# A gated short-convolution layer on one core: half of the weight remainders of the two-tile stage made by an adding DMA

## The chip, the core and the metric

The kernel runs on one core of a Trainium2 chip. The metric is the device time in microseconds of one execution. Engines are named as in the profile: PE multiplies matrices, PEld is its weight load, DVE, ACT and POOL are the vector, scalar and general engines, and SP issues most of the DMAs. "L314" is line 314 of the kernel before.

## The reference

With 256 tokens, a width of 2048 and a branch width of 4096, the reference does one layer: a normalisation with a modulation taken from a conditioning vector, a wide projection into four parts, a causal convolution of width three, two gates, a projection back, a gated residual and a second normalisation. Cut to what matters:

```python
h = rmsnorm(x, norm_g)
h, gate = adaln(h, c, ada_w, ada_b)              # h * (1 + scale) + shift
proj = einsum('bsd,de->bse', h, w_in)            # 2048 -> 4 * 4096
b_gate, c_gate, v, g = split(proj, 4)
u = causal_depthwise_conv(c_gate * v, conv_w)    # width 3
y = b_gate * u * silu(g)
x = x + gate * einsum('bse,ed->bsd', y, w_out)   # 4096 -> 2048
return rmsnorm(x, final_g)
```

All data is fp32. The kernel multiplies in the rounded type fp32r and keeps the accuracy by splitting each operand into a high part (the rounded value) and a low part (what the rounding left): a product is hi·hi + hi·lo + lo·hi.

## The kernel before, in words

The projection `w_in` is worked off in two stages, and the output projection is a third.

- The first stage (`mm_s` in the profile) takes the first 16 of the 32 column tiles of each quarter of `w_in`, four tiles at a time, in an order that a small planner writes out beforehand (`plan()`), together with the sums for the modulation. It ends at about 380 us of the span.
- The two-tile stage (`mm_b`), which the change touches, takes the other 16 column tiles of each quarter two at a time: `for ct in range(NS, NCT, 2)` makes 8 rounds, and in each the four quarters follow one another (`for q in QUARTERS`). One quarter of one round needs a slab of 2048 x 256 numbers of `w_in`, and it comes as two pieces of 1 MB (`for kp in range(0, KT, KP)` with `KP = 8`): the first piece has the upper 1024 rows (`kp == 0`), the second the lower 1024. So there are 64 pieces, 32 of them second ones.
- The output projection (`mm_o`) follows from about 730 us on.

A piece passes through four places in the two-tile stage. SP loads it into a tile `raw`. ACT rounds it to `hi` (`split_hi`, L314), DVE subtracts to get `lo = raw - hi` (`split_lo`, L319), and PE does 48 products of 128x128 weights and 256 tokens with it, two column tiles by 8 row blocks by 3 products, in the order hi, hi, lo for each block (`product`, L444). Then the quarter's PSUM bank is taken up by ACT or DVE (L595 to L606).

Each of the three kinds of tile has three buffers that turn round (`raw_tile`, `hi_tile`, `lo_tile`, each with `bufs=3`). So `hi` and `lo` of a piece can be written only when PE has ended the piece three back, and a `raw` load can start only when its old content has been read by both ACT and DVE. Inside this stage the order of the instructions on each engine is made by the framework's scheduler, by priorities and by its own idea of when things are ready; PE, ACT, DVE, POOL and SP each run their own list strictly in order and wait for semaphores.

Of the kernel before, what the change touches and what calls it, by code (L numbers as in the profile page):

```python
# [10 lines left out]
AF = mybir.ActivationFunctionType  # L11
ALU = mybir.AluOpType

P = 128
# [16 lines left out]
SLOT = 2048  # L31
# [86 lines left out]
def short_conv_layer(ctx: ExitStack, tc: tile.TileContext, x, c, norm_g, ada_w, ada_b, w_in, conv_w, w_out, final_g, out):  # L118
    nc = tc.nc
# [19 lines left out]
    def raw_tile(name):  # L139
        return wpool.tile([P, SLOT], F32, tag="raw", name=name, bufs=3)  # L140
# [165 lines left out]
    def hi_tile():  # L306
        return wpool.tile([P, SLOT], F32R, tag="hi", name="hi", bufs=3)

    def lo_tile(lo_tag="lo"):
        return wpool.tile([P, SLOT], F32R, tag=lo_tag, name="lo", bufs=3)  # L310

    def split_hi(raw, n, hi=None):
        hi = hi_tile() if hi is None else hi
        nc.scalar.copy(hi[:, :n], raw[:, :n])  # L314
        return hi

    def split_lo(raw, n, hi, lo_tag="lo", lo=None):
        lo = lo_tile(lo_tag) if lo is None else lo
        nc.vector.tensor_tensor(out=lo[:, :n], in0=raw[:, :n], in1=hi[:, :n].bitcast(F32), op=ALU.subtract)  # L319
        return hi, lo  # L320
# [13 lines left out]
    def split(raw, n, lo_tag="lo"):  # L334

        return split_lo(raw, n, split_hi(raw, n), lo_tag)
# [48 lines left out]
    def conv(ct, u, cv):  # L385

        nc.scalar.activation(u, cv, AF.Copy, scale=cw[:, 64 + ct : 65 + ct])
        nc.vector.scalar_tensor_tensor(
            out=u[:, 1:T], in0=cv[:, 0 : T - 1], scalar=cw[:, 32 + ct : 33 + ct], in1=u[:, 1:T], op0=ALU.mult, op1=ALU.add
        )  # L390
        nc.vector.scalar_tensor_tensor(
            out=u[:, 2:T], in0=cv[:, 0 : T - 2], scalar=cw[:, ct : ct + 1], in1=u[:, 2:T], op0=ALU.mult, op1=ALU.add
        )

    def split_y(dst, y):
        nc.scalar.copy(dst[:, :, 0, :], y)
        nc.vector.tensor_tensor(out=dst[:, :, 1, :], in0=y, in1=dst[:, :, 0, :].bitcast(F32), op=ALU.subtract)
# [42 lines left out]
    def product(dst, hi, lo, k, i, begins, left, ends):  # L440

        w, h = ((hi, hh_), (hi, hl_), (lo, hh_))[i]

        mm = last_mm[0] = nc.tensor.matmul(dst, w, h[:, k], start=begins and left, stop=ends, skip_group_check=True)  # L444
        if begins and left:
            opener[0] = mm
        elif begins:
            tc.add_manual_dep(mm.ins, opener[0].ins.name, after, reason="the bank's flags are cleared first")
# [97 lines left out]
    def gate_piece():  # L546
        if not gate_todo:
            return
        dc, j = gate_todo.pop(0)
        at = adap.tile([P, ASLOT], F32, tag="at", name="at_g", bufs=4)  # L550
        at3 = at.rearrange("p (k f) -> p k f", k=2)
        with later(GIVE):
            gate_sums(dc, j, at3)
# [17 lines left out]
    KP = 8  # L571
    n_piece = 0
    for ct in range(NS, NCT, 2):
        for q in QUARTERS:
            bank = psum.tile([P, CT, T], F32, tag="mm", name="mm_b")[:, 0:2]
            col = q * E + ct * P
            for kp in range(0, KT, KP):
                raw = raw_tile("raw")
                nc.sync.dma_start(
                    raw.rearrange("p (k f) -> p k f", k=KP),  # L580
                    w_in[0, kp * P : (kp + KP) * P, col : col + 2 * P].rearrange("(k p) f -> p k f", p=P),
                )
                hi, lo = split(raw, SLOT)
                for m in range(2):
                    for i in range(KP):
                        k = kp + i
                        o = slice((i * 2 + m) * P, (i * 2 + m + 1) * P)
                        for j in range(3):
                            product(bank[:, m, :], hi[:, o], lo[:, o], k, j, k == 0 and j == 0, m == 0, k == KT - 1 and j == 2)
                n_piece += 1  # L590
                if n_piece % 2 == 0:
                    gate_piece()
            z = zs[q // 2][:, q % 2]
            if q == 1:
                nc.scalar.copy(z, bank)  # L595
                zc = z
            elif q == 2:
                nc.vector.tensor_tensor(out=zc, in0=bank, in1=zc, op=ALU.mult)
                for j in range(2):
                    conv(ct + j, z[:, j, :], zc[:, j, :])  # L600
                u = z
            elif q == 3:
                nc.scalar.activation(z, bank, AF.Silu)
                nc.vector.tensor_tensor(out=u, in0=u, in1=z, op=ALU.mult)
            else:
                nc.vector.tensor_tensor(out=u, in0=bank, in1=u, op=ALU.mult)  # L606
                split_y(ys[ct // 2], u)
# [43 lines left out]
    for dc in range(4):  # L651
# [10 lines left out]
        for ep in range(n_ep):  # L662

            first = dc == 0 and ep == 0
            raw = wpool.tile([P, SLOT], F32, tag="raw" if first else "lo", name="raw_o", bufs=3)
# [10 lines left out]
            hi, lo = split(raw, SLOT, "raw")  # L676
# [55 lines left out]
```

## Time and profile before

| | before |
|---|---|
| time of the two runs | 913.66 us and 913.24 us (median 913.45 us) |
| the profiled execution's span, first to last instruction | 911.9 us |
| PE busy, instructions | 895.7 us (98%), 7047 |
| DVE busy, instructions | 616.2 us (68%), 593 |
| ACT busy, instructions | 464.6 us (51%), 413 |
| POOL busy, instructions | 0.7 us, 6 |
| HBM read | 224.49 MB |

The profile is of one execution; of that execution itself it gives the span, and the median of the two timed runs is 1.55 us above it. Busy time is summed per engine over the whole span. A PE that is busy all the time does not say that it is at its peak, but an engine that is never idle in a stage is one that no other engine has made wait there. In the views a row "A <- B" under waits means that A stood idle until B was done.

### The profile page before, as it was taken

Reading aid. Unit: us, or ns where it says so; the run is one execution under the profiler, and the core shown is the slowest. Engines: PE = TensorE matmul, PEld = TensorE weight load, DVE = VectorE, ACT = ScalarE, POOL = GpSimd, SP = SyncE. Lnnn points to the kernel's source line nnn. Section 1 sums busy time; section 2 is a strip of 40 time slices with the busy share of each in tenths; the row PEclk is TensorE's granted clock in tenths of the full one; section 3 lists DMA queues with packets and bytes.
Section 4 is the critical chain, followed back from the end, with each engine's and each line's share of the span. In section 5 each row is a group of like instructions: output and inputs, shape, how many; then the busy total and the mean of one; then the engine's idle time right before and its main releaser. Section 6 shows DMA issues by size and latency. Waiting matters only on the chain.

```text
span 911.9 us, 16239 instructions
## 1 busy us (share of the span) xinstructions
PE 895.7 (98%) x7047; PEld 858.5 (94%) x7047; DVE 616.2 (68%) x593; ACT 464.6 (51%) x413; POOL 0.7 (0%) x6
## 2 busy tenths in 40 slices
PE   6999999999999999999999999999999999999996
PEld 4999999999999999999999999999999988888885
DVE  4889999989888899765545555545554544555882
ACT  6768856665558756743334433444333333443333
POOL 0000000000000000000000000000000000000000
PEclk9999999999999999999999999999999999999998
DMA  9999999999998698676656665566656486655542
GB/s 309 367 371 353 365 325 351 356 369 352 338 328 275 197 359 301 201 246 197 186 188 197 200 201 186 187 195 200 200 188 188 140 331 231 203 201 186 185 139 92
DMA packets 163752, 227.65 MB, mean 250 GB/s; under 512 B 5680, under 2 KB 104160, under 8 KB 163296
## 3 DMA queue, kind: packets, MB, share of 16 engines
q1 hardware_dynamic: 163552, 226.56, 74.8%
q8 instruction: 55, 0.90, 0.4%
q14 instruction: 17, 0.14, 0.0%
q10 hardware_dynamic: 128, 0.04, 0.0%
HBM read 224.49 MB, written 2.10 MB: 248 GB/s over the span
## 4 chain that ended last, share of the span: by engine, by line
PE 94%; DMA 3%; ACT 1%; SPq 1%; DVE 0%; issue 0%; ACTq 0%
PE mm_b L444 38%; PE mm_s L444 36%; PE mm_o L631 6%; PE mm_o L629 6%; PE mm_o L630 6%; DMA raw_s<-in_sc_w_in_dram 2%; DMA at<-in_ada_w_dram 1%; SPq L210 1%; DMA x<-in_x_dram 1%; ACT hi L314 0%; PE ps_gate L568 0%; PE tp_g L434 0%; ACT acc L465 0%; DVE lo L319 0%; ACT hT L300 0%; SPq L413 0%
## 5 line engine op out<-in xcount | busy, mean ns | idle before, releaser
L444 PE MATMUL mm_s<-hT,hi 128*128 128x256 f32 x2048 | 350.5, 277 | 0.2
L444 PE MATMUL mm_b<-hT,hi 128*128 128x256 f32 x2048 | 348.8, 276 | 0.0
L444 PEld LDWEIGHTS mm_s<-hT,hi 128*128 128x128 f32 x2048 | 308.7, 188 | 1.1 <-ACT hT L300 0.4
L444 PEld LDWEIGHTS mm_b<-hT,hi 128*128 128x128 f32 x2048 | 308.7, 188 | 0.2 <-issue 0.2
L444 PE MATMUL mm_b<-hT,lo 128*128 128x256 f32 x1024 | 282.6, 276 | 0.0
L444 PE MATMUL mm_s<-hT,lo 128*128 128x256 f32 x1024 | 282.2, 277 | 0.2 <-DVE lo L319 0.2
L319 DVE TENSOR_TENSOR lo<-raw,hi 128x2048 fp32r<-128x2048 f32 (+1 forms) x66 | 148.0, 2244 | 136.8 <-ACT hi L314 136.8
L314 ACT CAST hi<-raw 128x2048 fp32r<-128x2048 f32 (+1 forms) x66 | 123.7, 1874 | 200.2 <-PE mm_b L444 156.1
L444 PEld LDWEIGHTS mm_b<-hT,lo 128*128 128x128 f32 x1024 | 192.2, 188 | 0.2 <-issue 0.2
L444 PEld LDWEIGHTS mm_s<-hT,lo 128*128 128x128 f32 x1024 | 191.7, 188 | 0.7 <-DVE lo L319 0.6
L319 DVE TENSOR_TENSOR lo<-raw_s,hi 128x2048 fp32r<-128x2048 f32 (+1 forms) x80 | 147.6, 1850 | 25.6 <-ACT hi L314 24.6
L314 ACT CAST hi<-raw_s 128x2048 fp32r<-128x2048 f32 (+1 forms) x80 | 124.2, 1559 | 72.0 <-PE mm_s L444 59.2
L319 DVE TENSOR_TENSOR lo<-raw_o,hi 128x2048 fp32r<-128x2048 f32 x32 | 73.3, 2292 | 66.3 <-ACT hi L314 66.1
L314 ACT CAST hi<-raw_o 128x2048 fp32r<-128x2048 f32 x32 | 61.0, 1907 | 107.2 <-PE mm_o L631 83.7
L630 PE MATMUL mm_o<-lo,y 128*128 128x512 f32 x256 | 99.7, 391 | 0.0
L629 PE MATMUL mm_o<-hi,y 128*128 128x512 f32 x256 | 99.3, 389 | 0.0
L631 PE MATMUL mm_o<-hi,y 128*128 128x512 f32 x256 | 99.3, 389 | 0.0
L427 DVE SCALAR_TENSOR_TENSOR gv<-at,silu_c,gv 128x512 f32<-128x512 f32 x105 | 78.6, 749 | 2.2 <-DMA at<-in_ada_w_dram 0.3
L465 ACT COPY acc<-mm_s 128x1024 f32<-128x1024 f32 x54 | 54.5, 1012 | 35.9 <-PE mm_s L444 35.9
L630 PEld LDWEIGHTS mm_o<-lo,y 128*128 128x128 f32 x256 | 48.1, 188 | 10.2 <-issue 0.2
L631 PEld LDWEIGHTS mm_o<-hi,y 128*128 128x128 f32 x256 | 48.0, 188 | 10.2 <-issue 0.2
L629 PEld LDWEIGHTS mm_o<-hi,y 128*128 128x128 f32 x256 | 48.1, 188 | 9.9
(89 smaller groups left out, 349.6 us busy)
## 6 DMA issues: line engine op xcount, KB each, us to landing
raw<-in_sc_w_in_dram SPq DMA_DIRECT2D x64, 1024.0 KB, 5.7
raw_s<-in_sc_w_in_dram SPq DMA_DIRECT2D x47, 1024.0 KB, 7.9
raw_o<-in_sc_w_out_dram SPq DMA_DIRECT2D x32, 1024.0 KB, 5.1
at<-in_ada_w_dram SPq DMA_DIRECT2D x114, 256.0 KB, 8.0
raw_s<-in_sc_w_in_dram SPq DMA_DIRECT2D x33, 512.0 KB, 7.1
at_g<-in_ada_w_dram SPq DMA_DIRECT2D x32, 512.0 KB, 7.8
at<-in_ada_w_dram SPq DMA_DIRECT2D x6, 512.0 KB, 9.6
x<-in_x_dram SPq DMA_DIRECT2D x4, 512.0 KB, 6.4
```

The source lines that it names most:

```text
L210: nc.sync.dma_start(at[:, :, s, :], adas[:, j : j + kk, s, 0 : NK0 * P])
L314: nc.scalar.copy(hi[:, :n], raw[:, :n])
L319: nc.vector.tensor_tensor(out=lo[:, :n], in0=raw[:, :n], in1=hi[:, :n].bitcast(F32), op=ALU.subtract)
L427: nc.vector.scalar_tensor_tensor(out=gv, in0=at4[:, i], scalar=c_k, in1=gv, op0=ALU.mult, op1=ALU.add)
L444: mm = last_mm[0] = nc.tensor.matmul(dst, w, h[:, k], start=begins and left, stop=ends, skip_group_check=True)
L465: nc.scalar.copy(acc[ch, q], bank)
L629: nc.tensor.matmul(po, yh, hi[:, o], start=opens, stop=False, skip_group_check=True)
L630: nc.tensor.matmul(po, yh, lo[:, o], start=False, stop=False, skip_group_check=True)
L631: nc.tensor.matmul(po, yl, hi[:, o], start=False, stop=ct == NCT - 1, skip_group_check=True)
```

## The change

In the two-tile stage the first piece of each quarter is handled as before. For the second piece (`kp` = 8) ACT writes `hi` as before, and then a second ACT instruction writes the rounded value once more, with the sign turned, into `lo`. A DMA that POOL issues then reads the same 1 MB of `w_in` from HBM a second time and adds it to what stands in `lo`, so that `lo` = -hi + raw. DVE's subtraction for these 32 pieces is gone. `lo` of a second piece is now written by ACT and then by the DMA, and PE's products with it wait for the DMA. Tiles, buffer counts and the loads by SP are as before.

```diff
                 raw = raw_tile("raw")
-                nc.sync.dma_start(
-                    raw.rearrange("p (k f) -> p k f", k=KP),
-                    w_in[0, kp * P : (kp + KP) * P, col : col + 2 * P].rearrange("(k p) f -> p k f", p=P),
-                )
-                hi, lo = split(raw, SLOT)
+                w_piece = w_in[0, kp * P : (kp + KP) * P, col : col + 2 * P].rearrange("(k p) f -> p k f", p=P)
+                nc.sync.dma_start(raw.rearrange("p (k f) -> p k f", k=KP), w_piece)
+                if kp == 0:
+                    hi, lo = split(raw, SLOT)
+                else:
+                    hi, lo = split_hi(raw, SLOT), lo_tile()
+                    nc.scalar.activation(lo, raw, AF.Copy, scale=-1.0)
+                    nc.gpsimd.dma_start(lo.rearrange("p (k f) -> p k f", k=KP), w_piece, accum_op=ALU.add)
```

## The prediction

> **What bounds the kernel now.** I read the page first, for the whole span: which engine is busy, and the chain of work that ended last.
>
> ```profile
> span 911.9 us, 16239 instructions
> PE 895.7 (98%) x7047; PEld 858.5 (94%) x7047; DVE 616.2 (68%) x593; ACT 464.6 (51%) x413; POOL 0.7 (0%) x6
> ...
> PE 94%; DMA 3%; ACT 1%; SPq 1%; DVE 0%; issue 0%; ACTq 0%
> ```
>
> The chain lies on PE for 94% of the span and on DVE for none, although DVE is busy for 68% of it. The change is confined to the two-tile stage, so I then asked for busy times by windows: first the stage, and below it a stretch early in the kernel, where the DMA engines are fullest. The columns are the window, its length, the busy time of PE, PEld, DVE, ACT and POOL with counts, the granted clock, the DMA share and GB/s.
>
> ```profile
> 380.00:729.00 349.00, 349.00 (x3076) 348.52 (x3076) 185.15 (x138) 142.21 (x106) 0.00 (x0) 1.00 0.61 194
> 20.00:60.00 40.00, 39.62 (x343) 38.88 (x342) 34.69 (x44) 30.66 (x39) 0.00 (x0) 1.00 1.07 368
> ```
>
> PE is busy in all 349.0 us of the stage, its weight load in 348.5, at the full clock. One product takes 349 / 3076 = 113.5 ns, and a piece of 48 products 5.45 us. DVE has 164 us of idle time in the stage and ACT 207. So nothing that is taken off DVE there can shorten the stage by more than half a microsecond; the question is whether the new way of making `lo` keeps up.
>
> How much room it has is read from the waits in this window and from ACT's timeline.
>
> ```profile
> ACT hi L314 <- PE mm_b L444: 162.6, 49, 4.4
> DVE lo L319 <- ACT hi L314: 138.7, 62, 3.1
> ...
> 478.32 1.91 ACT L314 CAST hi<-raw 128x2048 fp32r<-128x2048 f32 x1 [3.53 <-PE mm_b L444]
> 480.14 0.57 ACT L595 COPY z<-mm_b 128x512 f32<-128x512 f32 x1
> 483.72 1.91 ACT L314 CAST hi<-raw 128x2048 fp32r<-128x2048 f32 x1 [3.00 <-PE mm_b L444]
> 489.16 1.91 ACT L314 CAST hi<-raw 128x2048 fp32r<-128x2048 f32 x1 [3.53 <-PE mm_b L444]
> ```
>
> ACT's rounding waits for PE, not for the load: a `hi` buffer comes free when PE ends the piece three back, every 5.4 us (478.32, 483.72, 489.16), and the raw data is there. From that moment to PE's own use two whole pieces pass. Before, 1.91 us of ACT and 2.29 us of DVE had to fit into them, which leaves more than half of the room unused.
>
> **The change part by part.** What is removed and what ACT is given:
>
> ```profile
> L319 DVE TENSOR_TENSOR lo<-raw,hi 128x2048 fp32r<-128x2048 f32 x62 | 142.1, 2292 | 133.1 <-ACT hi L314 133.1
> L314 ACT CAST hi<-raw 128x2048 fp32r<-128x2048 f32 x62 | 118.6, 1913 | 197.3 <-PE mm_b L444 156.1 <-issue 40.7 <-PE mm_s L444 0.5
> ```
>
> DVE loses 32 subtractions of 2.29 us, 73 us; its stage sum falls from 185 to 112 us and the time gains nothing, because PE covers all of it. ACT gains 32 negated copies. Their shape and source are those of the rounding, so I take its 1.91 us: 61 us more, 142 to 203 of 349 us. That is hidden as a sum, but each copy stands ahead of the adding DMA and counts in its latency. Behind it in ACT's list stands the next piece's `hi`, which must wait for PE a piece longer anyway. The raw buffer is released by the copy instead of DVE's subtraction, 1.9 instead of 2.3 us after `hi`, so SP's loads start no later.
>
> The order of the changed program, which can be read without running it, moves PE's work as well. From about the tenth quarter on it repeats over two quarters: the first piece of quarter A (48 products), two `hi` products of A's second piece, 37 products of B's first piece, the other 46 of A's second piece, the last 11 of B's first, and the 48 of B's second. The earlier quarters interleave in a similar way. So A's second piece gets a late start, and B's second piece none.
>
> Now the room for each adding DMA, counted in PE's products. B's second piece takes the buffers of A's first piece, free after product 48, and its first `lo` product is number 146 (144 before it, two with `hi`): 98 products, 11.1 us. A's second piece takes the buffers of the previous B's first piece, free after product 144, and its `lo` is due at 192 + 87 = 279: 135 products, 15.3 us. ACT's `hi` (1.82 us from its start to the next instruction's in the timeline above) and the negated copy (1.91 us) come off both. What is left for POOL's wake-up, its issuing, the transfer and the semaphore is 7.4 us in the tight case and 11.6 us in the loose one. Call this latency L.
>
> If L is over 7.4 us, PE waits L - 7.4 us at B's second piece, once in two quarters, 16 times in 32 quarters. Every product behind it waits too, the next first piece with all its data ready among them, since PE's list is in order. That wait lengthens the loose room by as much, so the loose case never waits. The cost is 16 x (L - 7.4) us.
>
> L itself has no row, since no DMA in this trace adds and none comes from POOL. The nearest rows are SP's loads of the very same pieces, and the DMA queue in this window:
>
> ```profile
> L579 SPq DMA_DIRECT2D raw<-in_sc_w_in_dram x64: 367/368/379, 357.4 to 701.1; - x64
> ...
> DMA to landing us min/median/max: 5.3/5.7/9.7
> ...
> DMA packets 64300, 67.54 MB, mean 194 GB/s; under 512 B 1040, under 2 KB 62480, under 8 KB 64272
> ## 3 DMA queue, kind: packets, MB, share of 16 engines
> q1 hardware_dynamic: 64272, 67.11, 60.8%
> ```
>
> From below, the adding transfer cannot land sooner than a plain load of the same bytes in the same queues, 5.3 us: it would then be hidden and cost 0, and no gain lies below that since PE has no idle time to give. From above, take the slowest plain load, 9.7 us, twice, because the add needs the old `lo` from SBUF beside the new bytes from HBM: 19.4 us, or 16 x 12.0 = 192 us. Between them I take two median loads, 2 x 5.7 = 11.4 us: two reads for one write, and a queue that is shared with SP's loads. That gives 16 x (11.4 - 7.4) = 64 us.
>
> The Trainium skill's page "Collectives: The Full Stack", section "Why ReduceScatter is half of AllGather", says that an add in a DMA engine costs two read descriptors for each chunk and so half the rate, which is the doubling that I chose; no run here shows it yet. Its page "DMA: Bandwidth & Descriptors", section "Anatomy of one DMA — SWDGE (gpsimd) path", fits a POOL-issued DMA as 2.0 us plus its bytes at 436 GB/s: as an estimate 4.4 us for a plain megabyte and 6.8 us with the bytes counted twice, which would be hidden. The trace is against the fit's premise of free engines: its plain loads take 5.7 us with the engines 61% busy.
>
> The DMA engines set a second limit. The queue row gives 349 x 16 x 0.608 / 64272 = 52.8 ns for one packet of about 1 KB. The 32 adding DMAs bring 32 x 1024 = 32768 more of these. At one price each they need 108 us beside the 212 us of now, 320 of 349 us, and fit. At two they need 216 us, together 428 us: 79 us too many. With the full engines' price (368 GB/s in the early window, 16 engines, 44.5 ns) the same two come to 179 + 182 = 361 us, 12 us too many. These 12 and 79 us lie on both sides of the 64 us from the latency. They are another view of the same waits, so I do not add them.
>
> Issuing on POOL costs no one else anything, since POOL has no other work in the stage (0.00 us in the window). SP's list of loads keeps its order there.
>
> The sum is made against the profiled span: 911.9 + 64 = 976 us, and with the 1.55 us by which the median of the runs is above that span, **978 us**.
>
> **The rivals.**
>
> *Hidden.* The add's second read overlaps with the first, or the transfer's share of the engines is better than I think, and L stays under 7.4 us at both places. For it: a plain load lands in 5.3 to 5.7 us, and the DMA engines are idle for 39% of the stage. Against it: only 1.7 us would be left for the second read and for POOL's part. PE stays full and the time is 913 to 915 us; up to L = 8.5 us it would still be within 2%.
>
> *POOL is slow at issuing the rows.* Each of these DMAs has 1024 rows of 1 KB, and POOL has to issue them, which it does nowhere in this trace. Only one general instruction of POOL is there to price it:
>
> ```profile
> masks.py:199 POOL TENSOR_SCALAR_AFFINE_SELECT ident<-ident 128x128 f32<-128x128 f32 x1 | 0.3, 294 | 0.1
> ```
>
> That is 2.3 ns for an element; with 1024 rows and three records for each (two reads, a write) it makes 7.1 us. L would be 18.5 us, the cost 16 x 11.1 = 178 us and the time 1091 us. For it: nothing in the chain hides it. Against it: SP's issue of the same rows takes 0.37 us, and POOL may run ahead of the transfer.
>
> *The clock falls in the new waits.* After the last product, at about 904.4 us, the granted clock is
>
> ```profile
> 905.00:912.00 7.00, 0.00 (x0) 0.00 (x0) 1.31 (x3) 1.83 (x5) 0.00 (x0) 0.60 0.60 213
> ...
> 0.00:5.00 5.00, 0.26 (x1) 0.18 (x1) 0.17 (x2) 2.01 (x3) 0.70 (x6) 1.00 0.58 184
> ```
>
> If it falls to half, a mean of 0.60 means that it fell 2 us after PE stopped. Sixteen waits of 4 us could each be followed by some 2 us at half speed, losing 1 us each: 978 + 16 = 994 us. Against it: in the first 5 us of the kernel, the second row, PE is idle for 4.7 us and the clock stands at 1.00. The Trainium skill's page "TensorE: Matmul & The Clock Gate", section "Part 1: The HAM clock gate", says that an idle window of about 3.4 us halves the clock until another such window has been busy; that would be 1.7 us lost for each wait, as an estimate 27 us, and the end of this trace agrees that it falls.
>
> *Faster.* A shorter chain by way of DVE's relief would need a wait of PE on DVE in this stage, and PE has none; I give it the smallest chance.
>
> **How the numbers follow.** Waits of about 4 us at every second quarter, 978 us (own range 940 to 1030): 0.51. Hidden: 0.20. POOL slow or the add much dearer, around 1091 us: 0.18. The same as the forecast, with a falling clock, around 994 us: 0.10. Faster: 0.01. For eight times in ten I leave out half of the hidden case at the lower end and half of the slow case at the upper end: 918 to 1110 us. About 2% either way, 18 us, is what a measurement of this kernel can tell from no change. Within it lies the hidden case, 0.20; slower is the sum of the three others, 0.79; faster by more than that is 0.01.
>
> **What would show it right or wrong.** In the profile after, the waits should name PE on the DMA into `lo` about 16 times in the two-tile stage, for some 4 us each and 64 us together, and none of PE on DVE. The issue list should show 32 DMAs of 1 MB from POOL with a median of about 11 us to landing; 7 us or less is the hidden case, and 18 or more the slow one. ACT should show 32 negated copies of 1.9 us, and DVE's subtractions of `raw` should be 32 fewer. POOL's rows show whether its issuing takes tenths of a microsecond or several. The windows should keep the clock at 1.00, and the DMA share of the stage should rise to 0.9 or more. I am wrong about the mechanism if PE waits at every second piece instead of every other one, or if the waits fall on SP's `raw` loads.

## The result, and the profile after

The changed kernel takes 1026.42 us (two runs, 1026.39 and 1026.45) against 913.45 us: a ratio of 1.123, 95% interval 1.121 to 1.125. It is slower by 113 us; the forecast was slower by 64. The head of its page:

```profile
span 1024.7 us, 16353 instructions
PE 934.4 (91%) x7047; PEld 893.5 (87%) x7047; DVE 543.3 (53%) x561; ACT 520.9 (51%) x445; POOL 50.5 (5%) x38
...
PEclk9999999999999998898999898989999989999999
```

The last line needs care. It is the granted clock of PE in 40 slices of the span, and before the change it was

```profile
PEclk9999999999999999999999999999999999999998
```

After, the two-tile stage is a mixture of 9 and 8. PE makes the same 7047 products and is busy 38.7 us longer (934.4 - 895.7). The span grew by 112.8 us; the other 74 must be idle time of PE. The groups and the waits say where:

```profile
L444 PE MATMUL mm_b<-hT,lo 128*128 128x256 f32 x1024 | 297.7, 293 | 74.8 <-DMA lo<-in_sc_w_in_dram 65.5
...
PE mm_b L444 <- DMA lo<-in_sc_w_in_dram: 65.5, 14, 5.4
PE mm_b L444 <- ACT lo L585: 9.3, 2, 4.7
```

Ahead of `lo` products PE is idle for 74.8 us in 14 + 2 = 16 waits, none on DVE. The two that are put down to ACT's copy are of the same size and place; the DMA is what follows that copy. So 74.8 + 38.7 = 113.5 us accounts, within a microsecond, for the 112.8 us of the span. One of the waits, in the timelines of ACT, POOL and PE (start, duration, engine; the bracket is the idle time before):

```profile
580.07 1.91 ACT L585 ACTIVATE lo<-raw 128x2048 fp32r<-128x2048 f32 x1
...
582.34 1.55 POOL L586 DMA_DIRECT2D lo<-in_sc_w_in_dram  x1 [15.95 <-ACT lo L585]
...
588.94 0.28 PE L444 MATMUL mm_b<-hT,lo 128*128 128x256 f32 x1
589.05 0.39 PE L444 MATMUL mm_b<-hT,hi 128*128 128x256 f32 x2
594.05 0.40 PE L444 MATMUL mm_b<-hT,lo 128*128 128x256 f32 x1 [4.61 <-DMA lo<-in_sc_w_in_dram]
594.25 0.63 PE L444 MATMUL mm_b<-hT,hi 128*128 128x256 f32 x2
```

The copy ends at 581.98, and PE starts at 594.05: L is 12.1 us where 11.4 was taken, and 12.1 - 7.4 = 4.7 us fits the wait of 4.61. Behind it a product takes 0.40 us in the records where one ahead of it takes 0.28. By windows of 3.4 us across the wait before this one, and behind this one (us, PE, PEld, DVE, ACT, POOL, granted clock, DMA share, GB/s):

```profile
560.20:563.60 3.40, 0.00 (x0) 0.00 (x0) 2.89 (x2) 3.40 (x4) 0.00 (x0) 0.99 1.14 180
563.60:567.00 3.40, 2.16 (x10) 2.19 (x11) 0.00 (x0) 0.88 (x1) 1.55 (x1) 0.50 0.90 262
567.00:570.40 3.40, 3.40 (x18) 3.40 (x18) 0.00 (x0) 0.00 (x0) 0.00 (x0) 0.51 0.96 285
570.40:573.80 3.40, 3.40 (x32) 3.40 (x32) 0.00 (x0) 0.94 (x1) 0.00 (x0) 1.00 1.17 220
...
577.20:580.60 3.40, 3.40 (x33) 3.40 (x32) 0.00 (x0) 2.34 (x2) 0.00 (x0) 1.00 0.69 183
...
594.20:597.60 3.40, 3.40 (x17) 3.40 (x18) 0.00 (x0) 0.00 (x0) 1.57 (x1) 0.50 0.95 293
597.60:601.00 3.40, 3.40 (x32) 3.40 (x31) 0.00 (x0) 0.00 (x0) 0.00 (x0) 0.99 0.98 264
```

PE stands still for 4.7 us, then does 18 products in 3.4 us where 32 is usual, and the clock is back at 1.00 after 570. Behind the first wait two windows have half clock, behind the second one. Over the stage, 8 of the 16 waits have two such windows behind them and 8 have one, by the trace's clock records. The DMA share is 1.14 in the wait, but 1.17 again at 570.4 with PE busy, and 0.69 at 577.2. A share above 1 says that the recorded times of packets overlap, so it does not say by itself that nothing more would fit. The whole stage, its DMA queues, and the landing of the loads after:

```profile
380.00:848.30 468.30, 393.51 (x3105) 388.47 (x3104) 117.83 (x110) 200.03 (x142) 49.83 (x32) 0.91 0.95 218
...
q1 hardware_dynamic: 64800, 68.16, 49.1%
q0 software_dynamic: 33280, 33.56, 45.4%
...
raw<-in_sc_w_in_dram SPq DMA_DIRECT2D x60, 1024.0 KB, 6.6
lo<-in_sc_w_in_dram POOLq DMA_DIRECT2D x32, 1024.0 KB, 13.2
...
L586 POOL DMA_DIRECT2D lo<-in_sc_w_in_dram x32 | 49.8, 1557 | 775.0 <-ACT lo L585 775.0
```

The stage lasts 468 us instead of 349, and its DMA share rose from 0.61 to 0.95. Over 468 us on 16 engines, one packet of the adding queue (q0) takes 468 x 16 x 0.454 / 33280 = 102 ns, and one of SP's queue 56.7 ns (52.8 before): an adding packet costs 1.8 plain ones. The Trainium skill's page "Collectives: The Full Stack", section "Why ReduceScatter is half of AllGather", gives two read descriptors as the reason for a factor of two; this trace agrees in size.

### The profile page after: what moved, and what is told of

Read it like the earlier page. It is cut to its first block, busy times and chain, and to the rows that moved or that the text cites. A ratio compares the mean times of both kernels' runs of the same rounds, so it can differ in the third digit from the quotient of the medians.

```text
span 1024.7 us, 16353 instructions
## 1 busy us (share of the span) xinstructions
PE 934.4 (91%) x7047; PEld 893.5 (87%) x7047; DVE 543.3 (53%) x561; ACT 520.9 (51%) x445; POOL 50.5 (5%) x38
## 3 DMA queue, kind: packets, MB, share of 16 engines
q0 software_dynamic: 33280, 33.56, 20.8%
## 4 chain that ended last, share of the span: by engine, by line
PE 54%; issue 38%; POOL 4%; DMA 2%; ACT 1%; ACTq 0%; POOLq 0%; DVE 0%
PE mm_s L444 33%; PE mm_o L634 6%; PE mm_o L632 6%; PE mm_o L633 6%; POOL lo L586 4%; PE mm_b L444 2%; DMA lo<-in_sc_w_in_dram 1%; PE tp_idle L237 1%; DMA rows<-in_ada_b_dram 1%; PE sum L353 1%; PE tp_g L434 0%; PE tp_x L283 0%; ACT hi L314 0%; ACT acc L465 0%; PE ps_gate L568 0%
## 5 line engine op out<-in xcount | busy, mean ns | idle before, releaser
L444 PE MATMUL mm_b<-hT,hi 128*128 128x256 f32 x2048 | 379.6, 291 | 0.0
L444 PE MATMUL mm_b<-hT,lo 128*128 128x256 f32 x1024 | 297.7, 293 | 74.8 <-DMA lo<-in_sc_w_in_dram 65.5
L444 PE MATMUL mm_s<-hT,hi 128*128 128x256 f32 x2048 | 350.4, 277 | 0.1
L444 PEld LDWEIGHTS mm_b<-hT,hi 128*128 128x128 f32 x2048 | 334.1, 203 | 0.7 <-issue 0.5
L444 PEld LDWEIGHTS mm_s<-hT,hi 128*128 128x128 f32 x2048 | 308.3, 188 | 1.0 <-ACT hT L300 0.3
L444 PE MATMUL mm_s<-hT,lo 128*128 128x256 f32 x1024 | 282.1, 277 | 0.0
L444 PEld LDWEIGHTS mm_b<-hT,lo 128*128 128x128 f32 x1024 | 207.2, 203 | 77.7 <-ACT lo L585 34.5
L444 PEld LDWEIGHTS mm_s<-hT,lo 128*128 128x128 f32 x1024 | 191.8, 188 | 0.3
L319 DVE TENSOR_TENSOR lo<-raw,hi 128x2048 fp32r<-128x2048 f32 (+1 forms) x34 | 74.8, 2199 | 174.7 <-ACT hi L314 174.7
L586 POOL DMA_DIRECT2D lo<-in_sc_w_in_dram x32 | 49.8, 1557 | 775.0 <-ACT lo L585 775.0
L585 ACT ACTIVATE lo<-raw 128x2048 fp32r<-128x2048 f32 x32 | 61.1, 1909 | 0.0
L634 PEld LDWEIGHTS mm_o<-hi,y 128*128 128x128 f32 x256 | 48.0, 188 | 10.0
## 6 DMA issues: line engine op xcount, KB each, us to landing
lo<-in_sc_w_in_dram POOLq DMA_DIRECT2D x32, 1024.0 KB, 13.2
```

Of the source, the lines that this page charges most:

```text
L585: nc.scalar.activation(lo, raw, AF.Copy, scale=-1.0)
L586: nc.gpsimd.dma_start(lo.rearrange("p (k f) -> p k f", k=KP), w_piece, accum_op=ALU.add)
L634: nc.tensor.matmul(po, yl, hi[:, o], start=False, stop=ct == NCT - 1, skip_group_check=True)
```

## The experiments

The runs of the kernel before that stood beside these were between 913.4 and 913.8 us in the median. Ratios are to those. L444, L585 and L586 stay the names of the product, the negated copy and the adding DMA.

**1. The negated copy written ahead of the rounding** (`neg_first`).

```diff
-hi, lo = split_hi(raw, SLOT), lo_tile()
+lo = lo_tile()
 nc.scalar.activation(lo, raw, AF.Copy, scale=-1.0)
 nc.gpsimd.dma_start(lo..., w_piece, accum_op=ALU.add)
+hi = split_hi(raw, SLOT)
```

> ACT writes the negated copy, and POOL starts the adding DMA, ahead of the rounding instead of behind it, so the DMA starts some 1.8 us earlier. Theory A (the wait is latency minus room, and the half clock follows only from waits that are long enough to span a clock window): the changed kernel waits 16 times for about 4.7 us and shows half clock after each; each wait shrinks by 1.8 us to about 2.9 us, 46 us together, and since the drops in the changed kernel come in steps of 3.4 us, waits under 3.4 us leave the clock at 1.00. Time about 913.5 + 46 = 960 us, PE busy back near 896 us. Theory B (latency minus room, but any repeated wait brings the half clock): 1026 - 29 = 997 us, PE busy still near 934 us. Theory C (the DMA engines, 95% busy in the stage, are the bound): the transfer only gets longer, no change, 1020 to 1030 us.

1025.37 us, ratio 1.122 (1.120 to 1.124). The scheduler put the copy back behind `hi` on ACT, so this is the changed kernel again, and it tells nothing. Run 5 forces the order.

**2. The same DMA without the addition** (`plain_dma`).

```diff
-nc.gpsimd.dma_start(lo..., w_piece, accum_op=ALU.add)
+nc.gpsimd.dma_start(lo..., w_piece)
```

> The DMA from POOL copies instead of adding; lo then holds the raw weights, so the subtraction is left out. All waits, the second read of w_in from HBM and POOL's issuing stay. If the doubled reading of an adding packet makes the latency (packets of about 102 ns against 57 ns for SP's in the changed kernel): POOL's packets fall to about 53 ns, the transfer lands in 6 to 8 us instead of 11.7 us, which is at or under the room of 7.4 us, and the time is 913 to 925 us with the clock at 1.00. If POOL's queue itself (its 1.55 us of issuing, its path) makes the latency: landing stays at 10 us or more, and the time stays over 980 us.

957.09 us, ratio 1.048 (1.044 to 1.051), between the two expectations. This copy also changes the type, from fp32 to fp32r. The stage's DMA queues, and the groups:

```profile
q1 hardware_dynamic: 64534, 67.65, 56.0%
q0 software_dynamic: 33280, 33.56, 36.0%
...
lo<-in_sc_w_in_dram POOLq DMA_DIRECT2D x32, 1024.0 KB, 10.1
...
L444 PE MATMUL mm_b<-hT,lo 128*128 128x256 f32 x1024 | 284.0, 280 | 30.3 <-DMA lo<-in_sc_w_in_dram 30.0
```

A packet takes 396 x 16 x 0.360 / 33280 = 68.5 ns, and the 16 waits are 30.0 us in all. So taking the addition away gives back 69 of the 113 us; a second read of the weights from POOL's queue, even as a plain write, still costs 43. Landing in 10.1 us instead of SP's 5.7 to 6.6 us, it is not a "plain load" of the kind that bounded the forecast from below.

**3. ACT's part alone** (`dve_add`): the negated copy stays, and DVE adds `raw` to it.

```diff
-nc.gpsimd.dma_start(lo..., w_piece, accum_op=ALU.add)
+nc.vector.tensor_tensor(out=lo, in0=raw, in1=lo.bitcast(F32), op=ALU.add)
```

> The negated copy by ACT stays, but DVE adds raw to it in place of the DMA. This is ACT's part of the change alone, with DVE's old work. If the copies are hidden by PE as predicted: 913 to 915 us, PE never waits in the two-tile stage. If ACT's 61 us more cost something by their place in its list: 920 us or more.

913.87 us, ratio 1.0004 (0.9993 to 1.0014).

```profile
380.00:729.00 349.00, 349.00 (x3076) 348.52 (x3075) 186.19 (x140) 199.77 (x140) 0.00 (x0) 1.00 0.63 194
```

PE is as full as before, with 200 us of ACT in the window. The 61 us that ACT gained cost nothing, and neither does DVE's work in this place: what follows is the DMA's doing.

**4. More room: four `lo` buffers** (`four_lo`), on top of run 1. To make space the modulation's buffers are halved, which lengthens the first stage by 42 us; so the stage is compared, not the time.

```diff
-return wpool.tile([P, SLOT], F32R, tag=lo_tag, name="lo", bufs=3)
+return wpool.tile([P, SLOT], F32R, tag=lo_tag, name="lo", bufs=4 if lo_tag == "lo" else 3)
-at = adap.tile([P, ASLOT], F32, tag="at", name="at", bufs=4)      # and at_g
+at = adap.tile([P, ASLOT], F32, tag="at", name="at", bufs=2)
```

> As with the negated copy first, and lo has four buffers instead of three; the space comes from the buffers of the modulation weights, two instead of four, which may lengthen the first stage, so the two-tile stage is read by itself. The room grows by a whole piece, 5.4 us, to some 12.5 us after the copy; the transfers land after 11.6 to 14 us. Theory A: waits of 0 to 1.5 us, the two-tile stage within 349 to 375 us instead of 468 us, clock 1.00. Theory C (the DMA engines are the bound): the stage needs at least 64272 packets at 52.8 ns and 32768 at twice that over 16 engines, 428 us, whatever the room.

1034.17 us, ratio 1.131 (1.129 to 1.133). The two-tile stage by windows, its queues, and the landing:

```profile
422.70:850.70 428.00, 371.58 (x3076) 367.17 (x3075) 119.27 (x117) 203.58 (x145) 48.13 (x31) 0.95 1.04 241
...
q1 hardware_dynamic: 65837, 69.21, 54.5%
q0 software_dynamic: 33224, 33.50, 49.0%
...
raw<-in_sc_w_in_dram SPq DMA_DIRECT2D x61, 1024.0 KB, 12.7
```

The stage shrank from 468 to 428 us, the length expected of full DMA engines, and stopped far above 349: with the room widened, the DMA share is 1.04, and SP's loads take 12.7 us to land where they took 6.6 in the changed kernel. I read this as the transfers, and no longer one buffer, setting the pace.

**5. The copy forced ahead of `hi`** (`neg_forced`), which gives the 1.8 us of rounding back to the room.

```diff
+lo, hi = lo_tile(), hi_tile()
+neg = nc.scalar.activation(lo, raw, AF.Copy, scale=-1.0)
 nc.gpsimd.dma_start(lo..., w_piece, accum_op=ALU.add)
+high = nc.scalar.copy(hi, raw)
+tc.add_manual_dep(high.ins, neg.ins.name, after, reason="the negated copy first")
```

> The negated copy is now tied to stand ahead of the rounding in ACT's list (in neg_first the scheduler had put it behind again, so that kernel was the changed one over again). The scheduler drops the interleaving of PE's products with it: every second piece now has the same room, 11.1 us less one ACT instruction, 9.2 us. Latency theory with transfers of 11.6 us as in the changed kernel: each of the 32 second pieces waits about half of 12.0 - 9.2 us, 1.4 us, 45 us together; two-tile stage 394 us, time 958 us. Engine theory (an adding packet costs two plain ones, and the 16 DMA engines need 428 us for the stage): transfers get longer until the stage takes 428 us or a little more, the waits 79 us together and under 3.4 us each, time 993 to 1000 us. In both the clock stays at 1.00, if only waits over 3.4 us make it fall.

1001.29 us, ratio 1.095 (1.093 to 1.097). The scheduler also ceased to interleave the pieces on PE, so this isn't the room alone.

```profile
380.10:820.60 440.50, 380.56 (x3075) 376.00 (x3074) 114.92 (x108) 199.31 (x140) 48.14 (x31) 0.93 0.99 230
...
PE mm_b L444 <- DMA lo<-in_sc_w_in_dram: 59.9, 20, 5.2
```

The latency theory (958 us) falls, and the time is just above what was expected of the engines' limit (993 to 1000). The parts came otherwise, though: the waits are 59.9 us where that theory had 79, and PE's busy time is 32 us longer than before. The expectation that the clock would stay up was wrong: it is 0.93 in the stage.

**6. Half of the piece by the DMA** (`half_add`): DVE makes the first half of `lo`, ACT and the DMA the second.

```diff
+nc.scalar.activation(lo[:, HALF:], raw[:, HALF:], AF.Copy, scale=-1.0)
+nc.gpsimd.dma_start(lo[:, HALF:]..., w_piece[:, KP // 2 :, :], accum_op=ALU.add)
+nc.vector.tensor_tensor(out=lo[:, :HALF], in0=raw[:, :HALF], in1=hi[:, :HALF].bitcast(F32), op=ALU.subtract)
```

> The adding DMA makes only the second half of each second piece's lo (512 KB), and DVE subtracts the first half. Engine theory: the engines need 212 + 108 = 320 us of the 349 us, so they no longer set the pace, and the transfer lands in some 7 us, within the room: 913 to 925 us. If something fixed per DMA (issuing, waking, completion) were most of the latency, it would land after 10 us or more and the time would stay over 960 us.

930.97 us, ratio 1.019 (1.017 to 1.021), between the two expectations and the best version with an adding DMA.

```profile
q1 hardware_dynamic: 64272, 67.11, 62.8%
q0 software_dynamic: 16896, 16.78, 28.9%
...
lo<-in_sc_w_in_dram POOLq DMA_DIRECT2D x32, 512.0 KB, 9.7
...
L444 PE MATMUL mm_b<-hT,lo 128*128 128x256 f32 x1024 | 284.3, 278 | 11.3 <-DMA lo<-in_sc_w_in_dram 8.1
```

Half the bytes took 9.7 us to land, not the 7 that I had set. That is not a fixed part of L: the 512 KB adding DMAs of run 8 land in 7.5 us in the median. What makes the difference was not measured. A packet takes 366 x 16 x 0.289 / 16896 = 100 ns, as with the whole piece.

**7. Adding DMAs that nobody reads** (`add_unread`): DVE makes `lo` as before the change; ACT's copy and the adding DMAs, 512 KB each, go into spare buffers of the modulation (`at`).

```diff
+hi, lo = split(raw, SLOT)
+for s in range(2):
+    at = adap.tile([P, ASLOT], F32, tag="at", name="at_u", bufs=4)
+    nc.scalar.activation(at, raw[:, s * ASLOT : (s + 1) * ASLOT], AF.Copy, scale=-1.0)
+    nc.gpsimd.dma_start(at..., w_piece[:, s * 4 : s * 4 + 4, :], accum_op=ALU.add)
```

> lo is made by DVE as before the change. Beside it ACT still writes the negated weights and POOL still adds the same 32 MB to them, but into the buffers of the modulation weights, as two DMAs of 512 KB for each second piece, and nobody reads the sums. PE then waits for no adding DMA; what is left is the load on the DMA engines. Engine theory: the stage still takes 420 to 435 us, time about 990 us, and now it is SP's loads of raw that come late and ACT and PE that wait for them. Latency theory: PE is not touched, 913 to 916 us.

995.51 us, ratio 1.090 (1.087 to 1.092). The shared buffers also moved 30 loads of the modulation into the two-tile stage, so this run does not isolate the adding DMAs.

**8 and 9. The same with those loads kept early, and its copying twin** (`add_unread2`, `plain_unread`; the twin has no `accum_op`).

```diff
+while gate_todo:
+    gate_piece()          # ahead of the stage; the rest as in 7
```

> add_unread again without its confounder: there the buffers that the unread sums used delayed 30 loads of gate weights into the two-tile stage, 16 MB more and DVE behind them. Now those loads keep their old early place, and only the 32 MB of adding DMAs run beside the stage, unread. Engine theory (the stage needs about 428 us of the DMA engines): 980 to 1000 us, SP's raw loads late. Latency theory (only PE's waits for the adding DMA cost): 913 to 916 us. If the unread sums cost only part of the 79 us, the engines' limit is softer than two plain packets at 52.8 ns.

> As add_unread2, but POOL's DMAs copy instead of adding; the kernel's own result is whole. The same packets at one price: 212 + 108 = 320 us of the engines in a stage of 349 us. Engine theory: hidden, 913 to 918 us. If POOL's queue disturbs SP's loads by its mere presence: 925 us or more.

1016.84 us, ratio 1.115 (1.111 to 1.119), and 942.83 us, ratio 1.032 (1.030 to 1.034). Waits and landing of the adding one:

```profile
ACT at_u L589 <- DMA raw<-in_sc_w_in_dram: 244.9, 32, 11.7
...
PE mm_b L444 <- DVE lo L319: 45.6, 28, 1.8
...
DMA to landing us min/median/max: 5.8/7.5/14.0
```

Nobody waits for an adding DMA, and the kernel is still 103 us slower: ACT's copies stand in its list waiting for `raw`, which SP's queue delivers late, and the `hi` behind them is late in turn. But the twin loses 29 us with the same list, and its copies travelled as 9216 packets instead of 33792. So the 74 us between the two are the price of adding in small packets beside SP's loads in this arrangement, and not of the addition by itself. It is slower than run 7, so the moved loads were not what made that one slow.

**10. Forced order with idle products** (`neg_warm`): 5, and 20 products into an unused bank ahead of each second piece, some 2.4 us of them.

```diff
+for _ in range(20):
+    mm = nc.tensor.matmul(tp_warm[:, 0:T], hh_[:, 0, 0:P], hh_[:, 0, :], start=True, stop=True)
```

> neg_forced with 20 idle products (2.3 us) ahead of each second piece on PE, in the place where PE waits for the adding DMA, so that PE stays busy for most of the wait. In neg_forced PE waited 60 us and its busy time was 32 us longer by the half clock. If the half clock is on the path: the clock stays near 1.00 and the 32 us go, less what the idle products themselves delay: 970 to 985 us. If the DMA engines set the pace (428 us for the stage, 12 us less than neg_forced's 440 us): 988 to 1003 us, the idle products and the full clock only move time from one kind of waiting to another.

1004.43 us, ratio 1.099 (1.097 to 1.101), as in 5 without them. Twelve loads of the modulation moved into the stage as well.

```profile
378.20:821.30 443.10, 434.04 (x3719) 431.57 (x3718) 138.14 (x140) 199.26 (x140) 48.15 (x31) 0.99 1.03 243
...
PE mm_b L444 <- DMA lo<-in_sc_w_in_dram: 9.1, 5, 2.6
```

The clock is back at 0.99, and the stage is as long. The 640 idle products fill some 71 us of PE's list (2.23 us in each of 32 places); with the 9.1 us still idle that is 80 us, which has replaced 59.9 us of waits and some 20 of half clock. The DMA share is 1.03: the stage seems to wait for transfers whatever PE does, though the twelve loads add to them.

**11 and 12. The changed kernel's own PE order, with idle products in its 16 waits** (`order`, `order_warm`). The order of the changed kernel is written out by hand and chained, and the modulation's loads are kept early as in run 8; one of the two has 36 idle products in each of the 16 places where PE waits.

```diff
+run(eb, 11)                   # the end of B's first piece
+ob = piece(ct, qb, KP, bb)    # B's second piece
+run(ob, 2)
+for _ in range(WARM):         # 0 in order, 36 in order_warm
+    chain(nc.tensor.matmul(tp_warm[:, 0:T], hh_[:, 0, 0:P], hh_[:, 0, :], start=True, stop=True).ins)
+run(ob, 46)
```

> Control for the next: the changed kernel with PE's order of the two-tile stage written out by hand (48 products of quarter A's first piece, 2 of A's second, 37 of B's first, the other 46 of A's second, the last 11 of B's first, B's second), so that the scheduler cannot alter it; the gate sums are written ahead of the stage. It should behave as the changed kernel: 1020 to 1032 us, 16 waits of some 4.7 us at B's second piece, half clock behind each.

> The same order, with 36 idle products (4.1 us) on PE behind the two high products of B's second piece, where it waits for the adding DMA, so that no idle window is long enough to lower the clock; nothing else differs. If the half clock is on the path (the cost is the 75 us of waits plus 39 us of slow products): the clock stays at 1.00, the slow 39 us go, down to the engines' limit: 987 to 995 us. If the DMA engines alone set the pace already in the changed kernel: the waits grow by what the clock gives back, 1015 to 1030 us.

1032.62 us, ratio 1.131 (1.129 to 1.133), and 1006.67 us, ratio 1.102 (1.100 to 1.103). PE's row and the `lo` group, first of `order`, then of `order_warm`:

```profile
PE 933.0 (91%) x7047; PEld 891.9 (87%) x7047; DVE 542.8 (53%) x561; ACT 521.7 (51%) x445; POOL 50.5 (5%) x38
...
L444 PE MATMUL mm_b<-hT,lo 128*128 128x256 f32 x1024 | 298.5, 293 | 79.6 <-DMA lo<-in_sc_w_in_dram 70.5
```

```profile
PE 972.3 (97%) x7623; PEld 932.1 (93%) x7623; DVE 542.6 (54%) x561; ACT 521.9 (52%) x445; POOL 50.5 (5%) x38
...
L444 PE MATMUL mm_b<-hT,lo 128*128 128x256 f32 x1024 | 283.9, 279 | 15.7 <-DMA lo<-in_sc_w_in_dram 15.4
...
380.00:830.00 450.00, 432.69 (x3683) 427.68 (x3682) 119.04 (x112) 201.20 (x144) 49.82 (x32) 0.99 0.98 228
...
596.57 0.39 PE L444 MATMUL mm_b<-hT,hi 128*128 128x256 f32 x2
596.79 4.48 PE L644 MATMUL tp_warm<-hT 128*128 128x256 f32 x36
602.75 0.36 PE L444 MATMUL mm_b<-hT,lo 128*128 128x256 f32 x1 [1.48 <-DMA lo<-in_sc_w_in_dram]
```

In the place shown the 36 idle products fill 4.31 us, from 596.96 to 601.27; in all 16 places that is 69 us. With the 15.7 us still idle the gap is 85 us, 5 more than the 79.6 without them, and PE's busy time without the idle products fell from 933.0 to 903 us, by 30. The time fell by 26.0. So most of the half clock that was removed came off the time, and a little went into longer waits. That, and the 8 us by which PE is still above the 895.7 of before, is why the result lies between the two expectations. The order by itself is 6 us slower than the changed kernel.

## Why the prediction came out as it did

*What bounds the kernel: right.* PE was full and did not wait for DVE, so its relief gained nothing; ACT's copies cost nothing (run 3).

*Place and number of the waits: right.* There are 16, at B's second piece, on the adding DMA, and none in the loose case. L was 12.1 us against 11.4, and the waits were 74.8 us against 64, 17% above the forecast. The closeness is in part luck: the two halves of that guess were less sound than their sum. A copy from POOL into `lo` takes 10.1 us in the median, not the 5.3 us of the lower bound, and an addition of half the bytes 9.7 us there and 7.5 us in run 8. "Twice a plain load" hit the size of L without being how L comes about. POOL's DMAs also have a queue of their own (q0), where the prediction had one shared with SP's loads.

*The failed step is the clock.* It was set up as a rival to the forecast, "the same as the forecast, with a falling clock", with a chance of 0.10 and 1 us per wait; it should have been a term of the sum. Half clock after each wait added 38.7 us to PE's busy time over 16 waits, 2.4 us for each. The row of the first 5 us, quoted against it, was no evidence: the clock records of that trace begin 12 us into the span, so the 1.00 there has no record behind it. A group of twelve like products on both sides of that moment, the first four from 8.8 us on and the other eight from 12.3 us on, says the opposite:

```profile
L237 PE MATMUL tp_idle<-ones,ident 128*128 128x512 f32 x4 | 3.6, 1062 | 0.0
...
L237 PE MATMUL tp_idle<-ones,ident 128*128 128x512 f32 x8 | 3.6, 592 | 0.0
```

Four take 3.6 us and then eight do: the kernel before started at half speed. The Trainium skill's page "TensorE: Matmul & The Clock Gate", section "Part 1: The HAM clock gate", has windows of about 3.4 us; the windows above agree with that. The estimate of 27 us made from it, at 1.7 us for each wait, is below the measured 38.7, because half of the waits are followed by two such windows at half clock (563.6 to 570.4 us is one).

*"Another view of the same waits, so I do not add them": right for this kernel, but doubtful as a reading.* The engines' limit looks like a floor under the stage, and not like another view of the waits. The prediction had 428 us for the stage at two plain prices. Measured engine time (the shares of q1 and q0 by the window's length) in the stage, against its length:

| | q1 + q0 | window, us | engine time, us | stage, us |
|---|---|---|---|---|
| before | 60.8% | 349 | 212 | 349 |
| half_add | 91.7% | 366 | 336 | 365.5 |
| plain_dma | 92.0% | 396 | 364 | 395.5 |
| after | 94.5% | 468 | 442 | 468 |
| four_lo | 103.5% | 427 | 442 | 428 |

Half the added bytes give about half the added engine time. In the changed kernel the engine time is 26 us under the stage's length. More room (runs 4, 5) or a clock held up (10, 12) shortened the stage by 22 to 40 us, to shares of 0.98 to 1.04, and none came near 349 us. That full DMA engines stop it there is the reading that fits all of these, but no run shows it by itself. Where full is, is not sharp: run 4 has more engine time than stage, and run 7 has a share of 1.08 from 380 to 800 us.

*Rivals.* Hidden: fell, with L at 12.1 us. POOL slow at issuing: fell; it needs 1.55 us, not 7.1. Its time of 1091 us is farther from the result than 994, but the result lies between them. Faster: fell.

*The signs named.* Sixteen waits of 4 to 5 us and a DMA share over 0.9 came as said. The landing was to be about 11 us in the median and was 13.2, from 11.6 in the tight case to 16.2 in the loose one. "The windows should keep the clock at 1.00" did not: 0.91.

What stays open: how L is made up beyond its issue, and how much of the plain copy's 68.5 ns per packet is POOL's path rather than the change of type on the way. Neither was measured by itself. As an estimate, the 1024 rows of one DMA on 16 engines are 64 packets of 102 ns, 6.5 us of the 11.6 between issue and landing; the rest is not accounted for.

## What to carry to other kernels

Before an operation is moved from an engine with idle time to the DMA queues, take the price of its packets times their number and add it to the engine time of the stage: here 0.61 of the DMA engines were in use, and 32 MB of additions at 1.8 times the price had no room. Where a new wait of some 4 us stops PE, count the half clock behind it as a term beside the wait, and not as a case of its own. A relief for an engine that nobody waits for is worth nothing, so it must cost nothing.

## What was not expected of the hardware

- An adding packet of 1 KB takes 100 to 106 ns of a DMA engine in each kernel that has one; SP's plain loads of the same rows 51 to 57 ns; POOL's copy that changes fp32 to fp32r 68.5 ns.
- POOL's issue of 1024 rows takes 1.55 us for an addition and 0.88 us for the copy; SP's takes 0.37.
- POOL's copy from fp32 to fp32 went as 9216 packets for 33.56 MB, mostly 4 KB each; the one into fp32r kept 33280. The Trainium skill's page "DMA: Bandwidth & Descriptors", section "SWDGE vs HWDGE vs iDMA", says that a copy into fp32r always converts. That the conversion is what keeps the packets small was not tested.
- Waits of PE of 4 to 5 us are followed by one or two stretches of about 3.4 us at half clock. With 36 idle products in each wait the stage's granted clock is 0.99 instead of 0.91. Shorter waits are no guarantee: in run 2 the longest is 3.0 us, and three such stretches remain.
